# Leading loads issued in front of the entry barrier, and the first block loaded by four DMAs of every fourth partition

## Chip, cores and metric

The kernel runs on one core of one Trainium2 chip. The metric is the device time of one execution in microseconds (us). A page or view below that speaks of L71 or L73 means a line of the kernel's file.

## The reference

`x` is float32 of shape (32, 512, 1024), 67.1 MB; the result is 16,384 numbers:

```python
def reference(x: np.ndarray, multiplier: float) -> np.ndarray:
    return (np.sum(x, axis=-1) * multiplier).astype(np.float32)
```

## The kernel before

Each of the 128 partitions owns 128 neighbouring rows of `x` (512 KB). They are loaded in eight blocks of 16 rows; one block is 8 MB, and each partition's share of it is one contiguous run of 64 KB. Three buffers rotate. VectorE (DVE) reduces half of a block and ScalarE (ACT) the other half. The last block comes in shrinking pieces, so that little is left to compute when the last bytes land.

```python
    x_rows = x_flat.rearrange("(p c) d -> p c d", p=P)        # P = 128
    ...
    B = 16
    x_pool = ctx.enter_context(tc.tile_pool(name="x", bufs=3))
    ...
    for b in range(n_blocks - 1):                             # n_blocks = 8
        c0 = b * B
        t = x_pool.tile([P, B, D], fp32, name="xb")
        nc.sync.dma_start(out=t, in_=x_rows[:, c0 : c0 + B, :])
        h = B // 2
        nc.vector.reduce_sum(
            out=sums[:, c0 : c0 + h], in_=t[:, 0:h, :], axis=mybir.AxisListType.X
        )
        ...
        for r in range(h, B):
            act_row(t, r, c0 + r)
    ...                                                       # last block, in six pieces
    nc.sync.dma_start(out=out_view, in_=res)
```

The three buffers let three loads go at once, without waiting (three issues from 0.73 us in the timeline below). In the built program they follow the entry barrier, in which all engines meet after GpSimd (POOL) has written four small constants (the last write ends at 0.43 us).

## Time and profile before

| quantity | before | where it is read |
|---|---|---|
| time, median of 6 runs | 163.97 us | timed runs beside the change |
| span of the profiled run | 162.3 us | page |
| DMA engines busy | 96.5% | page, part 3 |
| DVE, ACT busy | 42% each | page, part 1 |
| first load issued | 0.73 us | timeline |
| first data moves | 1.74 us | packet records |
| a steady 64 KB packet | 2.42 us | packet records |
| last input lands | 159.06 us | landings in the trace |

The page of the kernel before; the row of digits is the busy share of the DMA engines in 40 slices, in tenths:

```profile
span 162.3 us, 234 instructions
DVE 68.2 (42%) x34; ACT 67.9 (42%) x127; POOL 0.2 (0%) x4
...
DMA  7979979979979979979989998998998997998990
...
q1 hardware_dynamic: 2016, 67.18, 96.5%
...
DMA 85%; DVE 11%; SPq 1%; issue 0%; DVEq 0%
```

The DMA engines are the limit, and they are almost saturated: 64 KB in 2.42 us is 27.1 GB/s per engine. The compute engines wait for data more than half the time (DVE 91.3 us, ACT 89.1 us of the 162.3). The chain that ended last (last line) is made of loads; the DVE share in it is two releases of a buffer (8.7 us each), at which two more blocks were already queued.

The end of that chain, in order of time (start us, length us, what): the last load that mattered, and DVE's first piece of work after it.

```profile
111.36 47.37 DMA xb<-in_x_dram
...
158.75 0.35 DVE xb L57
```

From there a fixed tail of 3.5 us follows: the last short DVE sums, the 64 KB store, the closing barriers. So a change at the start can only pay if the stream of loads ends earlier.

The start, in the timeline of the kernel before (start us, length us, engine, line, operation). "SPq" is the sequencer of SyncE, which issues the loads:

```profile
0.73 1.28 ACT L47 ACT_TABLE_LOAD   x1 [0.73 <-PEq L121]
0.73 1.33 SPq L71 DMA_DIRECT2D xb<-in_x_dram  x3
```

When do the 16 DMA engines begin? The windows view cuts the span into stretches of 0.25 us. Its columns are the stretch, its length, the busy time of DVE, ACT and POOL (with the number of instructions), the granted clock, the busy share of the DMA engines and GB/s. It books a packet where it starts, and one 64 KB packet in 0.25 us shows as 262 GB/s. The GB/s column (the last one) over 262 therefore counts the engines that begin their first packet in that stretch; a share above 1 has the same cause.

```profile
1.50:1.75 0.25, 0.00 (x0) 0.25 (x1) 0.00 (x0) 1.00 1.50 524
1.75:2.00 0.25, 0.00 (x0) 0.25 (x1) 0.00 (x0) 1.00 4.60 1573
2.00:2.25 0.25, 0.00 (x0) 0.01 (x1) 0.00 (x0) 1.00 1.53 524
2.25:2.50 0.25, 0.00 (x0) 0.00 (x0) 0.00 (x0) 1.00 0.76 262
2.50:2.75 0.25, 0.00 (x0) 0.00 (x0) 0.00 (x0) 1.00 2.15 786
2.75:3.00 0.25, 0.00 (x0) 0.00 (x0) 0.00 (x0) 1.00 1.30 524
```

That is 2, 6, 2, 1, 3 and 2 engines: sixteen starts, staggered over more than a microsecond (1.74 to 2.90 us in the packet records), the first a microsecond after the issue began (0.73 us).

### The profile page before, as it was taken

Reading aid. Unit: us, or ns where it says so; the run is one execution under the profiler, and the core shown is the slowest. Engines: PE = TensorE matmul, PEld = TensorE weight load, DVE = VectorE, ACT = ScalarE, POOL = GpSimd, SP = SyncE. Lnnn points to the kernel's source line nnn. Section 1 sums busy time; section 2 is a strip of 40 time slices with the busy share of each in tenths; the row PEclk is TensorE's granted clock in tenths of the full one; section 3 lists DMA queues with packets and bytes.
Section 4 is the critical chain, followed back from the end, with each engine's and each line's share of the span. In section 5 each row is a group of like instructions: output and inputs, shape, how many; then the busy total and the mean of one; then the engine's idle time right before and its main releaser. Section 6 shows DMA issues by size and latency. Waiting matters only on the chain.

```text
span 162.3 us, 234 instructions
## 1 busy us (share of the span) xinstructions
DVE 68.2 (42%) x34; ACT 67.9 (42%) x127; POOL 0.2 (0%) x4
## 2 busy tenths in 40 slices
DVE  0000039800596007940099101990049700697452
ACT  3000039700595007930099101990039600696870
POOL 0000000000000000000000000000000000000000
DMA  7979979979979979979989998998998997998990
GB/s 258 517 307 469 517 323 452 517 323 452 517 323 452 517 323 452 517 323 452 517 372 406 517 404 372 517 404 372 517 404 372 517 436 339 436 444 384 416 383 21
DMA packets 2017, 67.18 MB, mean 414 GB/s; under 512 B 224, under 2 KB 480, under 8 KB 736
## 3 DMA queue, kind: packets, MB, share of 16 engines
q1 hardware_dynamic: 2016, 67.18, 96.5%
q14 instruction: 1, 0.01, 0.0%
HBM read 67.11 MB, written 0.07 MB: 414 GB/s over the span
## 4 chain that ended last, share of the span: by engine, by line
DMA 85%; DVE 11%; SPq 1%; issue 0%; DVEq 0%
DMA xb<-in_x_dram 85%; DVE sums L73 11%; SPq L90 1%; DVE xb L57 0%; SPq L71 0%; DVE part L57 0%; DVEq L135 0%
## 5 line engine op out<-in xcount | busy, mean ns | idle before, releaser
L47 ACT ACTIVATE xb<-xb 128x1024 f32<-128x1024 f32 x63 | 65.6, 1042 | 89.1 <-DMA xb<-in_x_dram 89.1
L73 DVE TENSOR_REDUCE sums<-xb 128x8 f32<-128x8192 f32 x7 | 60.8, 8686 | 86.1 <-DMA xb<-in_x_dram 86.1
L47 ACT ACTIVATION_READ_ACCUMULATOR xb<-xb 128x1 f32 x63 | 11.7, 186 | 0.0
L57 DVE CUSTOM_DVE_ANT_0 xb<-xb 128x512 f32<-128x512 f32 (+1 forms) x9 | 5.8, 674 | 5.2 <-DMA xb<-in_x_dram 5.2
L47 ACT ACT_TABLE_LOAD x1 | 1.3, 1283 | 0.7 <-PEq L121 0.7
L76 DVE TENSOR_SCALAR res<-sums 128x8 f32<-128x8 f32 x7 | 1.2, 172 | 0.2
L57 DVE DVE_READ_ACCUMULATOR2_ANT res<- 128x1 f32 x9 | 0.7, 81 | 0.0
L57 DVE CUSTOM_DVE_ANT_0 xb<-xb,part 128x128 f32<-128x128 f32 x1 | 0.3, 350 | 0.0
L121 POOL MEMSET const-bfloat16-1.0<- 128x1 bf16 x1 | 0.1, 102 | 0.0
L121 POOL MEMSET const-uint8-127<- 128x1 uint8 x1 | 0.1, 102 | 0.0
L121 POOL MEMSET const-float32-1.0<- 128x1 f32 x1 | 0.1, 99 | 0.0
L121 POOL MEMSET const-float32-0.0<- 128x1 f32 x1 | 0.1, 98 | 0.2 <-issue 0.2
L57 DVE DVE_READ_ACCUMULATOR2_ANT part<- 128x1 f32 x1 | 0.1, 83 | 0.0
## 6 DMA issues: line engine op xcount, KB each, us to landing
xb<-in_x_dram SPq DMA_DIRECT2D x1, 4096.0 KB, 39.7
xb<-in_x_dram SPq DMA_DIRECT2D x1, 2048.0 KB, 44.2
xb<-in_x_dram SPq DMA_DIRECT2D x1, 1024.0 KB, 46.2
xb<-in_x_dram SPq DMA_DIRECT2D x1, 512.0 KB, 46.9
xb<-in_x_dram SPq DMA_DIRECT2D x1, 384.0 KB, 47.4
xb<-in_x_dram SPq DMA_DIRECT2D x1, 128.0 KB, 47.2
xb<-in_x_dram SPq DMA_DIRECT2D x7, 49.5
out_dram<-res SPq DMA_DIRECT2D x1, 64.0 KB, 1.5
```

The source lines that it names most:

```text
L47: nc.scalar.activation(out=t[:, r, :], in_=t[:, r, :], func=mybir.ActivationFunctionType.Copy, scale=mul, accum_out=res[:, col : col + 1],)
L57: nc.vector.tensor_tensor_reduce(out=t[:, r, lo:mid], in0=t[:, r, lo:mid], in1=t[:, r, mid:hi], scale=mul, scalar=start, op0=ADD, op1=ADD, ...
L73: nc.vector.reduce_sum(out=sums[:, c0 : c0 + h], in_=t[:, 0:h, :], axis=mybir.AxisListType.X)
L76: nc.vector.tensor_single_scalar(out=res[:, c0 : c0 + h], in_=sums[:, c0 : c0 + h], scalar=mul, op=mybir.AluOpType.mult,)
L90: nc.sync.dma_start(out=t[:, lo:hi, :], in_=x_rows[:, c0 + lo : c0 + hi, :])
L121: nc = _bacc.Bacc("TRN2", target_bir_lowering=False, num_devices=1)
```

## The change

The intent is to start the stream of loads earlier (no load at the head waits for anything, so it need not wait for the barrier) and to fill the 16 DMA engines sooner, by making the first DMA small: 32 rows, two 64 KB packets for each engine instead of eight (a block is 128 such packets in the trace; the share of each of the 16 engines is worked out, since the records name no engine). Rows are taken at a step of four.

```diff
-        nc.sync.dma_start(out=t, in_=x_rows[:, c0 : c0 + B, :])
+        step = 4 if b == 0 else 1
+        for q in range(step):
+            nc.sync.dma_start(
+                out=t[q:P:step], in_=x_rows[q:P:step, c0 : c0 + B, :]
+            )
 ...
+    def start_loads_at_entry(nc_):
+        entry, *rest = nc_.main_func.blocks
+        is_sp = lambda i: i.engine == mybir.EngineType.SP
+        is_load = lambda i: type(i).__name__ == "InstDMACopy"
+        for block in rest:
+            body = list(block.instructions)
+            own = [i for i in body if is_sp(i)]
+            if not any(is_load(i) for i in own):
+                continue
+            lead = []
+            for i in own:
+                if not is_load(i) or i.sync_info.on_wait:
+                    break
+                lead.append(i)
+            names = {i.name for i in lead}
+            block.instructions = [i for i in body if i.name not in names]
+            head = list(entry.instructions)
+            at = next(
+                k for k, i in enumerate(head) if is_sp(i) and type(i).__name__ == "InstDrain"
+            )
+            entry.instructions = head[:at] + lead + head[at:]
+            return
+
+    nc.at_finalize(start_loads_at_entry)
```

The added function moves the leading loads that wait for nothing (four DMAs of block 0, one each of blocks 1 and 2) in front of SyncE's drain, the first step of the entry barrier.

## The prediction

> **What bounds the kernel now.** The DMA engines. On the page they are busy 96.5% of the 162.3 us span, while DVE and ACT are busy 42% each; the chain that ended last is 85% "DMA xb<-in_x_dram". In the trace's packet records each of the 16 engines carries 56 packets of 64 KB plus the pieces of the last block, and a 64 KB packet takes 2.42 us (median and minimum). A block's load lands 49.5 us after its issue, so two blocks are always queued and no buffer wait starves the engines. The last input lands at 158.7 us, and the last DVE spans, the 64 KB store and the closing barriers take the other 3.5 us. Only an earlier or better filled start of the stream can move the end.
>
> **The start.** Timeline: SP's first load is issued at 0.73 us, after the entry barrier. Windows of 50 ns: no data before 1.70 us, then the 16 engines begin their first packets one after another, from 1.74 to 2.90 us, a spread of 1.16 us; these first packets take 3.05 us (early engines) down to 2.53 us (last), so first packets end between 4.79 and 5.43 us. At the end the landings of one piece still spread by 0.79 us, and the slowest engine sets the time.
>
> **What the change does.**
> 1. Moves the loads that wait for nothing (block 0 in four DMAs, blocks 1 and 2) in front of the barrier. First issue 0.73 -> about 0.0 us: -0.7 us, all on the critical path.
> 2. Block 0's first DMA has 32 rows, 2 packets per engine instead of 8. If the 1.16 us spread is the time to generate 128 rows' descriptors engine by engine, it falls to about 0.3 us (estimate, a quarter). Since first packets that start early take 3.05 us, I credit the slowest engine with only 0.3 to 0.6 us.
> 3. Adds three issues (0.33 to 0.50 us each in the trace) and 48 semaphore writes of 9 ns. Six issues hold SP about 2.6 us, so the barrier opens near 3.2 us instead of 0.65; block 0 lands at about 22 us, so none of this is on the path.
> 4. Tail unchanged.
>
> Sum: -1.0 to -1.3 us. Predicted 162.7 us, 8 in 10 between 162.1 and 163.5. Chances: faster by over 2%: 4%; within 2%: 91%; slower by over 2%: 5%.
>
> **What would show it.** First issue near 0 and first packets near 1.0 us (step 1); the 16 starts within 0.5 us, last landings closer together (step 2); barrier-end and table load near 3 us, no new wait on DVE or ACT (step 3); steady 64 KB packets still 2.42 us.
>
> **What would make it wrong.** [...] A SyncE drain in the barrier that waited for loads in flight would starve the DMAs. Or the starts are staggered by something other than row count: then only step 1 pays, about 163.2.

-0.7 us from step 1 and -0.3 to -0.6 us from step 2 make the -1.0 to -1.3 us. That the spread of the starts is time spent on the rows of the first DMA is step 2's assumption; no trace showed it, and the experiments test it.

## The result

| | before | the change |
|---|---|---|
| median of 6 runs | 163.97 us | 163.49 us |
| lowest to highest | 163.76 to 164.09 | 163.38 to 163.63 |
| ratio, with 95% interval | | 0.9972 (0.9959 to 0.9985) |
| span of the profiled run | 162.3 us | 161.6 us |

Ratios here and below are the mean time of one kernel's fast runs over the mean of the other's of the same rounds, so not quite the ratio of the medians.

The result is correct and the kernel is faster, clear of noise, but by 0.48 us where 1.0 to 1.3 us were forecast. That 163.49 us lies just inside the stated range (162.1 to 163.5) is luck: one step's gain and another's loss are added up in it, as the experiments show. The page of the changed kernel:

```profile
span 161.6 us, 243 instructions
DVE 68.2 (42%) x34; ACT 67.8 (42%) x127; POOL 0.2 (0%) x4
...
DMA  7998998998988988998998998998998997999990
...
q1 hardware_dynamic: 2064, 67.18, 96.8%
...
DMA 84%; DVE 11%; SPq 3%; issue 0%; DVEq 0%
```

Nothing of substance moved here. The end of the chain has the same parts as before, 0.59 us earlier:

```profile
110.77 47.37 DMA xb<-in_x_dram
...
158.16 0.31 DVE xb L57
```

The start has changed. The timeline of the changed kernel, loads alone:

```profile
0.00 3.73 SPq L73 DMA_DIRECT2D xb<-in_x_dram  x6
```

SyncE now issues from time zero, as forecast, but six issues take it 3.73 us. The same lines by source, before (L71) and after (L73), with the shortest, median and longest time of an issue in ns:

```profile
L71 SPq DMA_DIRECT2D xb<-in_x_dram x7: 327/328/426, 0.7 to 89.9; - x7
```

```profile
L73 SPq DMA_DIRECT2D xb<-in_x_dram x10: 327/493/764, 0.0 to 89.5; - x10
```

An issue of 32 strided rows is not quicker than one of 128 rows, but slower: 0.54 us for the first against 0.38 us before (the first SPq piece of each kernel's chain). And the windows of the changed kernel:

```profile
1.25:1.50 0.25, 0.00 (x0) 0.00 (x0) 0.00 (x0) 1.00 6.20 2097
1.50:1.75 0.25, 0.00 (x0) 0.00 (x0) 0.00 (x0) 1.00 1.58 524
1.75:2.00 0.25, 0.00 (x0) 0.00 (x0) 0.00 (x0) 1.00 0.81 262
2.00:2.25 0.25, 0.00 (x0) 0.00 (x0) 0.00 (x0) 1.00 2.32 786
2.25:2.50 0.25, 0.00 (x0) 0.00 (x0) 0.00 (x0) 1.00 1.37 524
```

Two things went against the forecast. The first data comes at 1.34 us, not at 1.0: of the 0.73 us by which the issue moved, the first data gained only 0.40. And the starts are as staggered as before: 8, 2, 1, 3 and 2 engines over 1.14 us.

Lastly, what waited on ACT in the changed kernel:

```profile
ACT L47 <- DMA xb<-in_x_dram: 22.8, 1, 22.8
```

The table load of ACT now comes behind waits for three of block 0's four DMAs, so it runs when they have landed (22.81 us, for 1.28 us) and ACT's first row starts 1.3 us after DVE's. This was not forecast either; it costs nothing, since ACT has that much slack in a block: it still waits 9.55 us for block 1.

### The profile page after: what moved, and what is told of

Its sections match the earlier page's. It is cut to its first block, busy times and chain, and to the rows that moved or that the text cites. A ratio compares the mean times of both kernels' runs of the same rounds, so it can differ in the third digit from the quotient of the medians.

```text
span 161.6 us, 243 instructions
## 1 busy us (share of the span) xinstructions
DVE 68.2 (42%) x34; ACT 67.8 (42%) x127; POOL 0.2 (0%) x4
## 4 chain that ended last, share of the span: by engine, by line
DMA 84%; DVE 11%; SPq 3%; issue 0%; DVEq 0%
DMA xb<-in_x_dram 84%; DVE sums L77 11%; SPq L73 2%; SPq L94 1%; DVE xb L57 0%; DVE part L57 0%; DVEq L167 0%
```

## The experiments

Theory A after the result: the early issue is worth its 0.7 us and more; the strided split costs about 0.3 us of it and gives nothing back. Rivals: the split is what pays (B); an issue in front of the barrier is slow whatever its shape (C); loads issued close behind one another hinder the first one's start (D).

### Early loads, block 0 in one DMA

```diff
-        step = 4 if b == 0 else 1
+        step = 1
```

> Only half of the change: the loads stand in front of the barrier, but block 0 is one DMA of 128 rows. Theory A (the split neither narrows the staggered start nor helps; its first issue of 542 ns against 377 ns even costs): first issue takes about 0.38 us, first data near 1.0 us, starts spread by 1.1 us, time 163.3 us or less, that is, as good as the change or better (ratio to before 0.995 to 0.997). Rival B (the split is what pays, the early issue gives only part): time 163.7 us or more, ratio above 0.998. Rival C (the place in front of the barrier, not the 32-row shape, makes the first issue long): first issue again 0.54 us and first data at 1.34 us.

Measured: 163.16 us against 164.05 us, ratio 0.9947 (0.9933 to 0.9960). The timeline's line of loads, and the windows:

```profile
0.00 1.32 SPq L73 DMA_DIRECT2D xb<-in_x_dram  x3
```

```profile
1.00:1.25 0.25, 0.00 (x0) 0.00 (x0) 0.00 (x0) 1.00 6.32 2097
1.25:1.50 0.25, 0.00 (x0) 0.00 (x0) 0.00 (x0) 1.00 1.59 524
1.50:1.75 0.25, 0.00 (x0) 0.02 (x1) 0.00 (x0) 1.00 0.76 262
1.75:2.00 0.25, 0.00 (x0) 0.25 (x1) 0.00 (x0) 1.00 2.19 786
2.00:2.25 0.25, 0.00 (x0) 0.25 (x1) 0.00 (x0) 1.00 1.33 524
```

The first issue takes 0.38 us, as after the barrier, and the first data comes at 1.00 us: the whole picture of before (2+6, 2, 1, 3, 2 engines), moved by 0.74 us. B and C fall. Half of the change is better than the whole of it.

### The split alone, after the barrier

```diff
-    nc.at_finalize(start_loads_at_entry)
```

> The other half alone: block 0 in four DMAs of every fourth partition, issued after the barrier. Theory A: starts of the 16 first packets still spread by about 1.1 us, first packets about 3.05 us, ratio to before 1.000 within 0.001; if the 32-row shape itself makes the issue long, its first issue takes about 0.54 us and the ratio is 1.001. Rival B: ratio about 0.998, with last landings 0.3 us earlier than before.

Measured: 164.16 us against 164.05, ratio 1.0006 (0.9993 to 1.0019). First issue 0.54 us, first data at 2.05 instead of 1.74 us, starts up to 3.45 us. The split alone gains nothing. That its first data is 0.31 us late doesn't show clearly in the time: the interval runs from 0.1 us faster to 0.3 us slower.

### Only block 0's load in front

The split is taken out as above, and the function moves one load only:

```diff
                 lead.append(i)
+                break
```

> Only block 0's load, unsplit, stands in front of the barrier; blocks 1 and 2 are issued after it (about 0.75 us later). Theory A: same time as the unsplit early loads, within 0.1 us. Rival D (issues that follow at once slow or stagger the first packets[...]): starts spread by clearly less than 1.1 us, or first packets clearly shorter than 3.05 us, and a time lower by 0.2 us or more.

Measured: 163.23 us against 164.05, ratio 0.9949 (0.9936 to 0.9962). Starts from 1.02 to 2.16 us, first packets 2.93 us on average. No difference from three loads in front: the gain needs one early load only, and D finds no support. It is not fully tested, though: the second issue still came at 0.77 us, before the first data.

### Four DMAs of 32 neighbouring partitions

```diff
-                out=t[q:P:step], in_=x_rows[q:P:step, c0 : c0 + B, :]
+                out=t[q * P // step : (q + 1) * P // step],
+                in_=x_rows[q * P // step : (q + 1) * P // step, c0 : c0 + B, :],
```

> As the change, but each of the four DMAs takes 32 neighbouring partitions instead of every fourth. [...] If the ports do not bind for this shape: block 0's packets stay at 2.42 us and the time is that of the change, 163.5 us.

Measured: 183.98 us against 164.05, ratio 1.1213 (1.1197 to 1.1228). Two stretches of this kernel's windows, the first while block 0 is loading, the second later (last column GB/s):

```profile
10.00:20.00 10.00, 0.00 (x0) 0.00 (x0) 0.00 (x0) 1.00 1.02 210
...
45.00:65.00 20.00, 9.76 (x3) 10.59 (x21) 0.00 (x0) 1.00 0.98 423
```

And the first stretch of the changed kernel:

```profile
10.00:20.00 10.00, 0.00 (x0) 0.00 (x0) 0.00 (x0) 1.00 1.00 433
```

All 16 engines are busy in both kernels (DMA share 1.02 and 1.00), and move half as much here, 210 against 433 GB/s: a 64 KB packet of block 0 takes 5.11 us (median) instead of 2.42. Block 0 lands at 43.35 instead of 22.72 us. The step of four avoids this. Of the two alternatives expected above, the second (2.42 us, 163.5 us) falls. What was measured is the rate by the partitions written. Two observations for later: the issue of 32 neighbouring rows took 0.38 us, and the starts spread over only 0.61 us (1.00 to 1.61).

### The change again, and two DMAs of every second partition

The change unaltered:

> The change itself again, to be compared on one chip with the other runs of this call and to have a second profile of it. The theory that the strided split costs about 0.3 us of the early start: ratio to before 0.997, first issue 0.54 us, first data at 1.34 us, as in its first profile. If the 0.9972 of its first measurement was drift between chips: 0.995, as the unsplit early load had.

Measured: 163.38 us against 163.99, ratio 0.9970 (0.9958 to 0.9983); first issue 0.55 us, first data at 1.33 us. The first result was no drift.

```diff
-        step = 4 if b == 0 else 1
+        step = 2 if b == 0 else 1
```

> Early loads, block 0 in two DMAs of every second partition (64 rows each). If the step between partitions makes the issue long, whatever the row count: each of the two issues takes 0.54 us or more, first data near 1.3 us, time about as the change (ratio 0.997). If it is the making of 128 single rows that takes time: a 64-row strided issue takes longer still, near 0.7 us. If only the number of issues matters: first issue 0.38 us, first data at 1.0 us, ratio 0.995. Packets of block 0 stay at 2.42 us [...].

Measured: 163.47 us against 163.99, ratio 0.9969 (0.9957 to 0.9981). Issues of 0.55 and 0.58 us, first data at 1.34 us; after the first, packets of block 0 stay at 2.42 us (446 GB/s from 10 to 20 us). 64 strided rows take as long to issue as 32 (0.54 and 0.58 us for the first two of the change): it is the step that costs, not the row count or the number of issues.

### A pitch of 508 KB between the partitions' rows

What staggers the starts? Here each partition takes 127 rows of `x`, so that the runs read in one DMA lie 508 KB apart instead of 512 KB, and one of the last 128 rows besides. The result is right. The core of the edit (the view `out_view` and the last block shift in the same way):

```diff
-    x_rows = x_flat.rearrange("(p c) d -> p c d", p=P)
+    R = rows - 1
+    x_rows = x_flat[0 : P * R].rearrange("(p c) d -> p c d", p=P)
+    x_extra = x_flat[P * R : N]
 ...
+        n = B if b else B - 1
+        nc.sync.dma_start(out=t[:, 0:n, :], in_=x_rows[:, c0 : c0 + n, :])
+        if b == 0:
+            nc.sync.dma_start(out=t[:, B - 1, :], in_=x_extra)
 ...
+        if b == 0:
+            nc.scalar.dma_start(out=out_extra, in_=res[:, R:rows])
```

> Tests what staggers the first packets. Each partition takes 127 rows of x, at a pitch of 508 KB instead of 512 KB, and one of the last 128 rows beside them (one more 512 KB load in front, one more small store early); right result, loads early and unsplit. Theory H (the 16 engines start at HBM addresses that differ by large powers of two and get in each other's way[...]): first packets spread over 0.5 us or less, first 64 KB-class packets near 2.42 us x 15/16 = 2.27 us instead of about 3.0 us, time 0.5 us or more below the unsplit early load (ratio 0.992 or less). Rival G (the engines are started one after another, about 70 ns apart, whatever they read): spread 1.1 us, first packets still about 0.6 us too long, ratio 0.995.

Measured: 165.59 us against 163.99, ratio 1.0107 (1.0071 to 1.0143), so slower, for a reason beside the question: while the little store of 4 bytes per partition had its turn (33 to 53 us), 46 of the 64 KB packets took 2.6 to 3.8 us instead of 2.42, and the store itself landed 24.0 us after its issue. That the store caused this is argued, not tested alone; but after 53 us, still at this pitch, a single packet took over 2.6 us, and a later run with this pitch in block 0, without the store, had nothing like it. The question got half an answer: the starts spread over 0.32 us (1.01 to 1.33) instead of 1.2, as H said, but the first packets got no shorter (3.11 us on average for 60 KB, where 2.27 us is steady), as G said. H's reason, that the addresses get in each other's way, is not shown by this. A run without the store was needed.

### The kernel before, a second profile

> The kernel before, for a second profile of it: how much of the difference between two profiles is chance. If the slow 64 KB packets outside the start (0.52 us per engine over the run before, 0.17 to 0.28 us in the four other kernels) belong to the kernel, they come again at 0.5 us; if they are chance, they are nearer 0.25 us. First issue 0.38 us, first data at 1.74 us, spread 1.1 us either way.

Measured: 164.12 us, one run. First data at 1.74 us, but the last engine started at 3.37 us: the stagger varies by chance, here 1.63 us. Slow packets after the start came to 0.18 us per engine instead of 0.52: these were chance too, and not a property of the kernel.

### Unsplit and split

The two kernels to compare, unaltered:

> The unsplit early loads again, beside the change on the same chip. Theory: ratio to before 0.995, and 0.2 to 0.4 us below the change of this call, because its first data comes at 1.00 us instead of 1.34 us and the first packets of its engines end 0.31 us earlier on average (4.48 against 4.79 us in the profiles so far). Rival: the gap of the two between different calls (0.9947 against 0.9972 and 0.9970) was chance, and both come out at 0.996 here.

> The change, in the same call as the unsplit early loads: ratio to before 0.997, 0.2 to 0.4 us above them; first issue 0.54 us, first data 1.34 us. The rival as told there: 0.996 for both.

Measured: 163.16 us, ratio 0.9947 (0.9934 to 0.9961), for the unsplit early loads; 163.60 us, ratio 0.9972 (0.9959 to 0.9985), for the change; 164.05 us for before. The gap of 0.44 us is a little above the 0.2 to 0.4 expected, and the intervals of the two, three of the change and two of the other, barely touch. Theory A holds in what it says of the time: the early issue pays, and the split costs. Why the split costs is a question for the next run. These are also the times of the version that beats both kernels.

### The step in SBUF without the step in HBM

A wrong result: written as in the change, but read from 32 neighbouring partitions' rows.

```diff
-                out=t[q:P:step], in_=x_rows[q:P:step, c0 : c0 + B, :]
+                out=t[q:P:step], in_=x_rows[q * P // step : (q + 1) * P // step, c0 : c0 + B, :]
```

> Wrong result on purpose: block 0 is written to every fourth partition in four DMAs, as in the change, but reads 32 neighbouring partitions' rows of x each time (row pitch 512 KB instead of 2 MB). If the step between the partitions written makes the issue long: first issue 0.54 us, first data 1.34 us, ratio 0.997. If the larger pitch of the rows read does it: first issue 0.38 us, first data 1.0 us, ratio 0.995. Packets stay at 2.42 us either way[...].

Measured: 163.19 us against 164.05, ratio 0.9947 (0.9933 to 0.9961). Neither expectation fits as a whole. Issues of 0.54 to 0.59 us and first data at 1.32 us: the step between the partitions written makes the issue long, as the first one said. Packets stay at 2.42 us: with the same rows read as in the neighbouring quarters (5.11 us), it was the partitions written that made those slow, not the reading. But the time is that of the unsplit loads. The windows show what else differs from the change:

```profile
1.25:1.50 0.25, 0.00 (x0) 0.00 (x0) 0.00 (x0) 1.00 9.63 3146
1.50:1.75 0.25, 0.00 (x0) 0.00 (x0) 0.00 (x0) 1.00 2.42 786
1.75:2.00 0.25, 0.00 (x0) 0.00 (x0) 0.00 (x0) 1.00 0.76 262
```

The starts come late but close together (12, 3 and 1 engines in 0.61 us), just as with the neighbouring quarters, which read the same rows. Same instruction shape and same number of rows as the change, other rows read: half the stagger, and 0.41 us less time. So the long issue and the late first data do not cost 0.4 us by themselves: here both are as in the change, and the time is not.

### The pitch of 508 KB alone

A wrong result: the unsplit early loads, with block 0 read at the other pitch and nothing else changed (`x_skew` is a view of 127 rows per partition).

```diff
+    x_skew = x_flat[0 : P * (rows - 1)].rearrange("(p c) d -> p c d", p=P)
 ...
-                out=t[q:P:step], in_=x_rows[q:P:step, c0 : c0 + B, :]
+                out=t[q:P:step], in_=(x_skew if b == 0 else x_rows)[q:P:step, c0 : c0 + B, :]
```

> Wrong result on purpose: as the unsplit early loads, but block 0 reads its 64 KB rows at a pitch of 508 KB instead of 512 KB, with no other load or store added. From the earlier run at this pitch: the starts of the 16 first packets spread over about 0.3 us instead of 1.2 us, at 1.0 to 1.35 us. Theory (the spread is no cost in itself, because the first packets of engines that start early are slowed until all are served): the average end of the first packets moves by less than 0.2 us from 4.48 us, and the ratio is within 0.0015 of the unsplit early load's. Rival (my prediction's step 2: narrowing the spread pays 0.3 to 0.6 us): ratio 0.993 or less.

Measured: 163.38 us against 164.05, ratio 0.9963 (0.9948 to 0.9978).

```profile
1.00:1.25 0.25, 0.00 (x0) 0.00 (x0) 0.00 (x0) 1.00 9.99 3146
1.25:1.50 0.25, 0.00 (x0) 0.00 (x0) 0.00 (x0) 1.00 0.73 262
```

Only 13 starts stand in these two lines; the other three fell just before 1.00 us. The spread is 0.36 us, and yet the time is no better than with 1.2 us (it misses the expected nearness by a hair, on the slow side). The first packets took 3.33 us on average instead of 3.05, and ended between 4.12 and 5.00 us, about as unsplit. A narrow start alone pays nothing.

## Why the prediction was wrong

The runs at 64 KB per packet can be put side by side. These numbers are worked out from the packet records (the start and length of the first packet of each engine) and the landings of the trace, in us:

| kernel | first start | last start | slowest first packet ends | last input lands | difference of the last two |
|---|---|---|---|---|---|
| before, two profiles | 1.74, 1.74 | 2.90, 3.37 | 5.53, 5.79 | 159.06, 159.13 | 153.5, 153.3 |
| split alone | 2.05 | 3.45 | 6.03 | 159.03 | 153.0 |
| the change, three profiles | 1.34, 1.33, 1.41 | 2.48, 2.18, 2.94 | 5.44, 5.30, 5.54 | 158.43, 158.32, 158.63 | 153.0, 153.0, 153.1 |
| early, every second partition | 1.34 | 2.22 | 5.49 | 158.75 | 153.3 |
| early, one DMA, two profiles | 1.00, 0.99 | 2.22, 2.17 | 4.87, 4.79 | 158.08, 158.21 | 153.2, 153.4 |
| only block 0 early | 1.02 | 2.16 | 4.98 | 158.10 | 153.1 |
| early, step in SBUF only | 1.32 | 1.93 | 5.01 | 158.14 | 153.1 |
| early, pitch 508 KB | 0.99 | 1.35 | 5.00 | 158.28 | 153.3 |

The last column is nearly constant, 153.0 to 153.5 us: in these profiles the end of the slowest engine's first packet tells, to within 0.5 us, when the last input lands. The column alone doesn't settle that this is the right measure, since from the first start to the last landing it is 156.8 to 157.4 us, hardly a wider range.

Two comparisons say more. The run with the step in SBUF only starts about as late as the change (1.32 against 1.33 to 1.41 us) and lands earlier (158.14 against 158.32 to 158.63): the first data alone doesn't decide. The pitch of 508 KB has less than a third of the unsplit load's spread and lands no earlier: nor does the spread alone. And the packets can be followed, each from the end of the one before (the records name no engine, and ends within 5 ns of each other can be swapped): the engine whose first packet ended last was last or last but one at the end of its 56th packet in eight of these twelve profiles, and among the last five of 16 in all. So the measure is well supported, not proved. (The prediction put the slowest end before the change at 5.43 us, from the last start; it is 5.53, of another engine.) By that measure the early unsplit load gains 0.7 to 1.0 us over before, and the change 0.0 to 0.5.

Point by point:

- **What bounds the kernel: right.** DMA engines saturated, tail unchanged, compute beside the path in every run.
- **Step 1 ("First issue 0.73 -> about 0.0 us: -0.7 us, all on the critical path"): right for the early issue itself.** Alone it moved the first data by 0.74 us and the time by 0.89 us (difference of the medians), within the interval of about 0.2 us either way.
- **Step 2 is the step that failed: "If the 1.16 us spread is the time to generate 128 rows' descriptors engine by engine, it falls to about 0.3 us ... I credit the slowest engine with only 0.3 to 0.6 us."** The spread stayed at 1.14 us with 32 rows in the first DMA (0.85 and 1.54 in two further profiles), and was 0.36 us with 128 rows at a pitch of 508 KB. So the number of rows alone doesn't set it; which rows are read together matters. That making descriptors takes this time, no trace shows. With the same rows-per-DMA and the same issue time, neighbouring rows gave 0.61 us and every fourth row 0.85 to 1.54. That the number plays no part is not shown: of neighbouring rows 512 KB apart, 32 gave 0.61 us and 128 gave 1.14 to 1.63. Nor does a narrower spread always pay: it came with 0.41 us less in one run (step in SBUF only, against the change) and with nothing in another (508 KB, against the unsplit load). The term credited with -0.3 to -0.6 us measured about +0.4 us (the change against the unsplit early loads, 163.60 against 163.16; behind the barrier, the split against before, 0.1 us with an interval from -0.1 to +0.3).
- **What stood in its place:** the step between partitions makes an issue last 0.54 us instead of 0.38, and the first data comes 0.31 to 0.34 us later (in front of the barrier and after it, with 32 and with 64 rows). The prediction costed the added issues from issues without a step, "0.33 to 0.50 us each", and held them to be off the path as a whole. The first of the six is not: it delays the first data. Only half of the 0.34 us is the longer issue; the rest lies between its end and the first data (0.62 us without the step, 0.38 to 1.00; 0.80 us with it, 0.54 to 1.34), and no run says where. But this delay is not shown to be the price: with it, the run with the step in SBUF only took 163.19 us, as the unsplit loads did (163.16). What took the price away there was to read rows 512 KB apart instead of 2 MB apart in each DMA: there the slowest first packet ended at 5.01 us, and in the change, as late and more staggered, at 5.30 to 5.54.
- **Step 3: the conclusion right, the sizes not.** The barrier opened at 4.06 us (SyncE's instruction records), not 3.2, since the issues were longer, and ACT's table load waited for block 0, to 22.81 us. Both are off the path, as said.
- **The fear that block 0's packets would be slow didn't come true:** with every fourth partition 64 KB packets stayed at 2.42 us, with 32 neighbouring partitions they took 5.11. Nor did the drain wait for loads in flight: the barrier opened (4.06 us) over 18 us before block 0 landed (22.72 us).
- **The fallback named at the end ("then only step 1 pays, about 163.2") describes the unsplit early loads, 163.16 us, exactly;** it missed that the split has a price.

What stays open: why starts are more staggered when the rows of a DMA lie 512 KB or 2 MB apart than 508 KB; how much of the split's price is the late first data and how much the stagger; why the first packets take about 3 us however they start (2.8 to 3.3 us on average, at each pitch and number of rows that ran at the full rate, where a steady 64 KB packet takes 2.42); and why bunched starts paid with the step in SBUF but not at the pitch of 508 KB. The end of the slowest first packet says that they did, 5.01 against 5.30 to 5.54 us for the change, and 5.00 against 4.79 and 4.87 for the unsplit load, but not by what.

## What to carry to other kernels

In a stream that keeps the DMA engines full (96.5% busy here), look at the end of the slowest engine's first packet to see what an earlier start is worth, and not only at the time of the first issue: here the last landing followed it to within 0.5 us. Issue the first load before anything that it does not need, in its plainest form: one DMA over 128 partitions without a step (163.16 us here, 163.60 with the step of four). Before cutting a DMA to fill engines sooner, test what the stagger depends on; and when partitions are cut, let every part reach over all of them, as the step of four does: parts of 32 neighbouring partitions cost 20 us here (183.98 us, with 64 KB packets of 5.11 us instead of 2.42).
